# A two-layer hybrid trunk: the RWKV preparation spread into even steps with a third stage, and the weight split and own-shift product moved to other engines

## The chip, the cores and the metric

The kernel runs on one core of a Trainium2 chip. TensorE (PE) does the matrix products, VectorE (DVE), ScalarE (ACT) and GpSimd (POOL) the element work, and SyncE (SP), ACT and POOL issue DMAs. The metric is the device time of one execution in microseconds (us); a kernel's time is the median of its runs. One execution of each kernel is also profiled, and all the rows below are of that execution.

## The reference, cut to what matters

Two layers run over 256 context tokens and 2048 latent tokens of width 1024. Each layer is, for all 2304 tokens:

```python
h = rms_norm(x, norm_w[l]) * (1.0 + scale) + shift        # scale, shift, gate from SiLU(c) @ mod_w
pa, pb, pt = _split(h @ w_in[l], (RWKV_COLS, HGRN_COLS, ATTN_COLS))
pa = pa + mu_prev * (prev(pa) - pa) + mu_next * (next(pa) - pa)      # centred_shift, RWKV columns only
...                                                       # RWKV-7, HGRN2 and windowed attention
x = x + gate * (jnp.concatenate([ya, yb, yt], axis=-1) @ w_out[l])
```

In the RWKV group a state of 64 by 64 for each of 6 heads and 2 directions is stepped through all tokens. The kernel does that in chunks of 64 tokens. For each chunk it needs products of decays, two triangular 64 by 64 matrices and the inverse of a unit triangular one, and these depend on the features alone, not on the state.

## The kernel before, in words

A layer has two phases. `inproj_phase` computes `h @ w_in`; `phase2` runs the three mixers and the output projection. The program's instructions are put in an order on each engine by a scheduler that works through the program as written and has a timing model of its own; an instruction that stands earlier in the program goes first when several could go. Each engine then executes its list strictly in that order, so what the scheduler placed too early makes the engine wait.

**The input projection.** The 4096 columns of `w_in` are worked in 32 columns of 128 (33 in layer 1, which has one more for `vw1`), in two sweeps over the tokens: sweep 0 has three groups of tokens (512, 256 and 512), sweep 1 has two of 512. For each position of a sweep `prefetch` splits the next column's weights `wraw` into `whi` and `wlo` (`split`, L307 to L314: a cast and a subtraction on POOL), and has POOL issue the load of the column after that into the one `wraw` buffer. `group` (L339) then runs 24 matmuls into a PSUM tile `ps` and has ACT empty it. For the 14 RWKV columns (`j < 14`, "shifted") ACT writes a padded row buffer `pb`, of which there is one, and `end` (L379) makes the centred shift out of it on DVE: `s = pb * mu0` (L391, `self.ts`), then two `self.stt` that add the neighbours' shares. For the other columns ACT writes `s` directly. Of `s` there are two buffers; `post` works on `s` and stores it to scratch in HBM.

**The preparation** (`RwkvPrep`, L608) makes the chunks' products window by window, 256 tokens each, 9 windows a layer, 5 in sweep 0 and 4 in sweep 1. `fronts` loads `th` (by an SP DMA from scratch `wa`) and `lr`, `lk`, `lkk`, casts `th` to `tk` (L699), multiplies by `wa` into PSUM `aps` on PE, goes through tanh, a scan and exponentials, forms `tk` and `lkk`, stores them, and multiplies them into the triangular matrices `M`. `backs` sends the diagonal 32 by 32 blocks of `M` through HBM (scratch `Lx`) into `inv` and `can`, inverts them by a chain of 60 small DVE instructions, copies the results on ACT, sends them through HBM again (scratch `Dx`, the writes on ACT's queue, the reads into `XT` and `daT` on SP's), and completes the inverse by two sets of 48 matmuls with operands of 32 by 32 each (as many for either direction): first `G = apm<-daT,M`, copied by ACT to `Gs`, then `apm<-XT,Gs`. `XT` goes to scratch `XD`.

Both are generators that `yield` between pieces. `advance` (L654) runs one piece of the back of one window and one of the front of another. `behind` (L400), called after every position, opens the preparation after position 9 of sweep 0 and adds the sweep's windows there, and calls `advance` `CFG["pa"]` = 6 times a position. Before, a window's front has five pieces for each direction, and its back five in all.

**Modulation.** In layer 0 the later shifts and gates (`later_modulation`) are computed among the first positions, at a priority lowered by `CFG["mo"]` = 1000 places. The preparation can be opened only when the modulation has released its PSUM and SBUF.

**Phase 2** is a merge of generators for the RWKV state, HGRN, attention and read-out. Attention begins by finishing what is left of the preparation and then takes its memory.

Of the kernel before, what the change touches and what calls it, by code (L numbers as in the profile page):

```python
# [17 lines left out]

CFG = dict(og=0, eg=0, ib=2, lo=0, xb=4, hf=3, np=3, tm=4, pa=6, ch=1, pq=2, wps=2, ahead=100, he=92, ae=86, re=105, mo=1000, hd=1, wq=2, rq=0, oq=0, rl=500, nx=0, nl=2, bl=2, xa=0, od=3, g1=0, g2=0, g3=0, b2=0, b3=0)
L = 2  # L20
# [22 lines left out]
def W(ap, n):  # L43
    return ap[:, n:n + 1]


class Trunk:
# [227 lines left out]
    def inproj_phase(self, l, src, prep, start):  # L275
# [7 lines left out]
        with ExitStack() as ph:  # L283
# [23 lines left out]
            def split(n):  # L307
                if n < len(seq):
                    w = raw.pop(n)
                    hi = wsp.tile([128, KD, 128], F32R, name="whi", tag="whi")  # L310
                    lo = wsp.tile([128, KD, 128], F32R, name="wlo", tag="wlo")
                    nc.gpsimd.tensor_copy(hi, w)  # L312
                    self.tt(lo, w, hi.bitcast(F32), ALU.subtract, nc.gpsimd)
                    spl[n] = (hi, lo)  # L314
# [24 lines left out]
            def group(sw, n, st, t0, bn, every):  # L339
# [17 lines left out]
                if not shifted:  # L357
                    self.evac(l, j, s[:, t0 - base:t0 - base + bn], ps[:, 0:bn], t0 - base, bn)
                else:
                    o = t0 - base + (1 if t0 == 0 or sw else 2)  # L360
                    if c0 == 0:
                        self.act(pb[:, o:o + bn], ps[:, 0:bn], AF.Identity)
                    if t0 == 0:
                        self.act(pb[:, 1282:1283], ps[:, BLK:BLK + 1], AF.Identity)

            edge = (nc.gpsimd, nc.vector)[CFG["eg"]]
# [12 lines left out]
            def end(sw, n, st):  # L379
# [3 lines left out]
                if shifted:  # L383
# [3 lines left out]
                    else:  # L387
                        segs = [(1280, 1024, 1)]
                    m0, mp, mn = W(self.mu0[l], j), W(self.P(l, "mup"), j), W(self.P(l, "mun"), j)
                    for t0, bn, c in segs:  # L390
                        sv = s[:, t0 - base:t0 - base + bn]  # L391
                        self.ts(sv, pb[:, c:c + bn], m0, ALU.mult)
                        self.stt(sv, pb[:, c - 1:c - 1 + bn], mp, sv, ALU.mult, ALU.add)
                        self.stt(sv, pb[:, c + 1:c + 1 + bn], mn, sv, ALU.mult, ALU.add)
# [5 lines left out]
            def behind(sw, pos):  # L400
                if sw == 0 and pos < 7:
                    next(start, None)
                if pos == 9:
# [204 lines left out]
class RwkvPrep:  # L608
# [3 lines left out]
    def __init__(self, t, l, ph):  # L612
        self.t, self.l, self.nc, self.ph = t, l, t.nc, ph
        self.todo, self.ready, self.done, self.front, self.back = [], [], set(), None, None

# [38 lines left out]
    def advance(self):  # L654

        if not self.front and self.todo:
            w = self.todo.pop(0)
            self.front = [w, self.fronts(w)]
        if not self.back and self.ready:
            w = self.ready.pop(0)  # L660
            self.back = [w, self.backs(*w)]
        if not (self.front or self.back):
# [12 lines left out]
    def fronts(self, w):  # L675
# [7 lines left out]
        def load():  # L683
            for n in ("r", "k", "kk"):
# [3 lines left out]
                nc.sync.dma_start(out=d[n], in_=S[n][:, :, t0:t0 + 256].rearrange("i p t -> p i t"))  # L688
        M = T_([128, 6, 4, 64], "M", 2)
        v3 = lambda a: a.rearrange("p i (c s) -> p (i c) s", s=64)  # L690
        f3 = lambda a: a.rearrange("p (c s) -> p c s", s=64)
        for z in range(2):
# [53 lines left out]
            nc.sync.dma_start(out=S["KB"][z, 4 * w:4 * w + 4].rearrange("c p i s -> p i c s"), in_=tk.rearrange("p (i c) f s -> p i c (f s)", c=4))  # L746
            for p0, pn in ((0, 2), (2, 1)):
                ps = self.ps([128, 8, 64])
# [11 lines left out]
    def backs(self, w, M):  # L760
# [5 lines left out]
        for z in range(2):  # L766
            for g, b in enumerate((0, 1) if z == 0 else (1, 0)):
# [15 lines left out]
        for j in range(1, 31):  # L783
# [3 lines left out]
            t.tt(i3[:, j + 1:32, 0:j], i3[:, j + 1:32, 0:j], tv, ALU.subtract)  # L787
        yield

# [3 lines left out]
        Dx = S["Dx"]  # L793
        daT = T_([128, 12, 32], "daT")
        for q in range(4):
# [5 lines left out]
            for hp in range(2):  # L801
# [3 lines left out]
                if g == 0:  # L805
                    nc.sync.dma_start(out=daT[rb], in_=Dx[4 + z, 12 * hp:12 * hp + 12].rearrange("u r c -> r u c"))
        yield

        G = self.pm.tile([128, 12, 32], F32, name="apm", tag="apm")
        Gs = T_([128, 384], "Gs").rearrange("p (u s) -> p u s", s=32)  # L810
        q4 = lambda hp, i: slice(64 * hp + 32 * i, 64 * hp + 32 * i + 32)
        for z in range(2):
            a, b = (0, 1) if z == 0 else (1, 0)
            for u in range(12):
                p, c = divmod(u, 4)
                for hp in range(2):
                    t.mm(G[q4(hp, b), u], M[q4(hp, a), 3 * z + p, c, 32 * b:32 * b + 32], daT[q4(hp, a), u])
        t.act(Gs, G, AF.Identity)
        yield
        O = self.pm.tile([128, 12, 32], F32, name="apm", tag="apm")  # L820
        for z in range(2):
            a, b = (0, 1) if z == 0 else (1, 0)
            for u in range(12):
                p, c = divmod(u, 4)
                for hp in range(2):
                    t.mm(O[q4(hp, a), u], Gs[q4(hp, b), u], XT[q4(hp, b), 3 * z + p, c, 32 * b:32 * b + 32])
        for z in range(2):
# [823 lines left out]
```

## Time and profile before

| | |
|---|---|
| median of 3 runs | 4546.02 us (4545.11 to 4547.92) |
| the profiled execution | 4540.61 us, span of the trace 4538.8 us |
| TensorE busy with matmuls / with weight loads | 3941.3 us (87%) / 3217.7 us (71%) |
| VectorE / ScalarE / GpSimd busy | 3164.2 us (70%) / 1984.9 us (44%) / 1390.9 us (31%) |
| mean granted TensorE clock | 0.929 of full speed |

Layer 0's input projection lies from the start to about 1230 us, its phase 2 to about 2290 us, layer 1's input projection to about 3495 us, and its phase 2 to the end. The preparation runs from about 350 to 800 us (sweep 0) and from 800 to 1230 us (sweep 1) in layer 0, and from 2500 to 2960 us and from 3160 to 3495 us in layer 1. The shares are averages over these stages; what the change touches is read from the input projections.

### The profile page before, as it was taken

To read this page: it belongs to the slowest core of one execution; us is meant where nothing else is said; L and a number is where in the kernel's file an instruction comes from. 1 tells how busy PE (TensorE), PEld (TensorE's weight loads), DVE (VectorE), ACT (ScalarE), POOL (GpSimd) and SP (SyncE) were. 2 spreads that over 40 slices of the span, in tenths; PEclk is the share of its full clock that TensorE was granted. 3 is DMA by queue.
4 is the path that set the end of the run, shared out by engine and by line. 5 is a ranking of instruction groups with operands and counts; after the bars stand their busy time and mean duration, and the time that the engine had idled before them with its cause. 6 is when DMAs were issued, how large, how long until landed. Compare 5 with 4: busy or idle time off the path is not lost. (4 is left out here: it accounts for less than half of the span.)

```text
span 4538.8 us, 98552 instructions
## 1 busy us (share of the span) xinstructions
PE 3941.3 (87%) x39424; PEld 3217.7 (71%) x39424; DVE 3164.2 (70%) x5646; ACT 1984.9 (44%) x4050; POOL 1390.9 (31%) x1298
## 2 busy tenths in 40 slices
PE   7998898889789889868979988898887888988788
PEld 4767776777677777766758767776676777777676
DVE  3547777678577887777744777556775877777786
ACT  3414343443355555533424353333433555555443
POOL 2322233223233332242243212243222422333232
PEclk8999898999899999988989989899898999999899
DMA  5466654666643334346634476435665543334554
GB/s 202 144 200 197 198 158 121 190 197 190 167 123 107 106 105 115 91 118 214 209 117 129 143 231 195 116 106 172 197 185 159 135 113 101 97 104 126 171 187 132
DMA packets 777312, 688.41 MB, mean 152 GB/s; under 512 B 352164, under 2 KB 675044, under 8 KB 776856
## 3 DMA queue, kind: packets, MB, share of 16 engines
q1 hardware_dynamic: 747624, 583.93, 43.4%
q0 software_dynamic: 18720, 68.17, 5.2%
q10 hardware_dynamic: 10512, 30.02, 2.0%
q8 instruction: 312, 5.11, 0.5%
q14 instruction: 144, 1.18, 0.1%
HBM read 440.70 MB, written 241.22 MB: 150 GB/s over the span
## 5 line engine op out<-in xcount | busy, mean ns | idle before, releaser
L67 PE MATMUL ps<-h,whi 128*128 128x512 f32 x4160 | 1374.7, 406 | 18.2 <-ACT s L64 11.2
L67 PEld LDWEIGHTS ps<-h,whi 128*128 128x128 f32 x4160 | 806.0, 195 | 207.7 <-issue 19.5
L67 PE MATMUL ps<-h,wlo 128*128 128x512 f32 x2080 | 850.9, 409 | 5.2 <-POOL wlo L74 5.2
L312 POOL CAST whi<-wraw 128x1024 fp32r<-128x1024 f32 x130 | 151.6, 1166 | 1124.0 <-PE ps L67 991.8
L67 PEld LDWEIGHTS ps<-h,wlo 128*128 128x128 f32 x2080 | 411.7, 198 | 95.4 <-POOL wlo L74 6.3
L74 POOL TENSOR_TENSOR hE<-hb 128x256 f32<-128x256 f32 x408 | 290.9, 735 | 326.7 <-PE wps L67 195.7
L74 POOL TENSOR_TENSOR wlo<-wraw,whi 128x1024 fp32r<-128x1024 f32 x130 | 335.3, 2579 | 10.5
L1085 DVE COPY_PREDICATED hatt<-lm,wps 64x256 f32<-64x256 int32 x476 | 266.7, 560 | 29.8 <-PE wps L67 23.2
L64 ACT ACT_TABLE_LOAD x177 | 227.1, 1283 | 109.9 <-DVE s L79 33.4
L74 DVE TENSOR_TENSOR Gs<-can,inv 128x30 f32<-128x30 f32 (+9 forms) x540 | 238.9, 442 | 35.0 <-PE apm L67 23.7
L67 PE MATMUL pq<-KZ,BKs 128*64 128x128 f32 x2496 | 228.2, 297 | 34.9 <-DMA KZ<-scr_RK 18.8
L67 PE MATMUL opo<-wohi,ohi 128*128 128x512 f32 x544 | 216.2, 413 | 31.2 <-DVE og L74 18.6
L74 DVE TENSOR_TENSOR hQz<-hE,hqz 128x512 f32<-128x512 f32 x204 | 179.8, 882 | 76.4 <-DMA hqz<-scr_hq 67.8
L74 DVE TENSOR_TENSOR inv<-inv,Gs 128x30 f32<-128x30 f32 (+9 forms) x540 | 223.5, 414 | 12.1
L83 DVE SCALAR_TENSOR_TENSOR s<-pb,par,s 128x1024 f32<-128x1024 f32 (+1 forms) x156 | 217.3, 1393 | 5.6
L67 PE MATMUL opo<-wolo,ohi 128*128 128x512 f32 x544 | 212.9, 407 | 0.0
L64 ACT ACTIVATE pt<-wps 128x512 f32<-128x512 f32 (+1 forms) x288 | 149.4, 525 | 137.1 <-PE wps L71 132.7
L67 PEld LDWEIGHTS pq<-KZ,BKs 128*64 128x64 f32 x2496 | 169.4, 147 | 53.6 <-issue 19.8
L64 ACT ACTIVATE s<-ps 128x512 f32<-128x512 f32 (+1 forms) x175 | 95.8, 562 | 251.6 <-PE ps L67 222.8
L64 ACT ACTIVATE pb<-ps 128x512 f32<-128x512 f32 (+2 forms) x162 | 77.1, 492 | 290.5 <-PE ps L67 204.1
L71 PE MATMUL wps<-ident,prob 128*128 128x128 f32 x960 | 168.7, 292 | 40.8 <-DVE hatt L1085 22.8
L79 DVE TENSOR_SCALAR s<-pb,mu 128x1024 f32<-128x1024 f32 (+1 forms) x78 | 62.1, 796 | 194.7 <-ACT pb L64 193.9
(272 smaller groups left out, 9225.8 us busy)
## 6 DMA issues: line engine op xcount, KB each, us to landing
wraw<-in_w_in_dram POOLq DMA_DIRECT2D x128, 512.0 KB, 4.6
scr_KB<-tk SPq DMA_DIRECT2D x36, 768.0 KB
BKs<-scr_KB SPq DMA_DIRECT2D x144, 192.0 KB
KZ<-scr_RK SPq DMA_DIRECT2D x272, 96.0 KB
x<-in_mod_w_dram SPq DMA_DIRECT2D x32, 512.0 KB
lkk<-scr_kk SPq DMA_DIRECT2D x36, 384.0 KB
th<-scr_wa SPq DMA_DIRECT2D x36, 384.0 KB
scr_RK<-lkk SPq DMA_DIRECT2D x36, 384.0 KB
```

What stands on the lines that cost most here:

```text
L64: return self.nc.scalar.activation(out=out, in_=in_, func=func, **kw)
L67: return self.nc.tensor.matmul(out=out, lhsT=lhsT, rhs=rhs, start=start, stop=stop)
L71: return self.nc.tensor.transpose(out, in_, self.ident[0:p, 0:p])
L74: return (eng or self.nc.vector).tensor_tensor(out=out, in0=a, in1=b, op=op)
L79: return e.tensor_scalar(out=out, in0=a, scalar1=s1, scalar2=None, op0=op0)
L83: return (eng or self.nc.vector).scalar_tensor_tensor(out=out, in0=a, scalar=s, in1=b, op0=op0, op1=op1)
L312: nc.gpsimd.tensor_copy(hi, w)
L1085: nc.vector.copy_predicated(o, m, d)
```

## The change

Five things change.

1. **Where the preparation's steps stand.** `advance` is called once after each `group` (three a position in sweep 0, two in sweep 1) and, by `behind`, one time more a position in sweep 1, so that a position has 3 calls and not 6, and they stand between its groups and not after it.
2. **Its pieces.** A front has six pieces for each direction and not five (the products into `M` are a piece of their own). The 60 instructions of the inversion are cut into pieces after `j` = 6, 12, 18, 24 and 30. What follows the second trip through HBM (`G`, its copy, the last products and the store to `XD`) becomes a third generator, `tails`, which `advance` runs beside the next window's back; it begins with four empty pieces, and there are two between `G` and the last products. `G`'s copy goes into free blocks of `M` and not into `Gs`.
3. **The weight split** goes from POOL to ACT (`whi`) and DVE (`wlo`).
4. **The own-shift product** `s = pb * mu0` goes from DVE (from `pb`, 128x1024 and 128x256 at a time, after the last group) to ACT (from PSUM, after each group).
5. **The later modulation** is lowered by 300 places and not by 1000.

```diff
-                    nc.gpsimd.tensor_copy(hi, w)
-                    self.tt(lo, w, hi.bitcast(F32), ALU.subtract, nc.gpsimd)
+                    self.act(hi, w, AF.Identity)
+                    self.tt(lo, w, hi.bitcast(F32), ALU.subtract)
...
                     if c0 == 0:
                         self.act(pb[:, o:o + bn], ps[:, 0:bn], AF.Identity)
+                        self.act(s[:, t0 - base:t0 - base + bn], ps[:, 0:bn], AF.Identity, scale=W(self.mu0[l], j))
...
+                prep.advance()
...
-                        self.ts(sv, pb[:, c:c + bn], m0, ALU.mult)
                         self.stt(sv, pb[:, c - 1:c - 1 + bn], mp, sv, ALU.mult, ALU.add)
                         self.stt(sv, pb[:, c + 1:c + 1 + bn], mn, sv, ALU.mult, ALU.add)
...
-                for _ in range(CFG["pa"]):
+                for _ in range(3 - (2 if sw or last and order[pos] in free else 3)):
                     prep.advance()
...
+        if self.tail and next(self.tail[1], 1) == 1:
+            self.done.add(self.tail[0])
+            self.tail = None
         if self.back and next(self.back[1], 1) == 1:
-            self.done.add(self.back[0][0])
+            self.tail = [self.back[0][0], self.tails(*self.back[0], *self.back[2:])]
             self.back = None
...
             t.tt(i3[:, j + 1:32, 0:j], i3[:, j + 1:32, 0:j], tv, ALU.subtract)
-        yield
+            if j % 6 == 0:
+                yield
...
-        yield
-
+
+    def tails(self, w, M):
+
+        t, nc, S = self.t, self.nc, self.t.scr
+        XT, daT = self.XT, self.daT
+        yield
+        yield
+        yield
+        yield
         G = self.pm.tile([128, 12, 32], F32, name="apm", tag="apm")
-        Gs = T_([128, 384], "Gs").rearrange("p (u s) -> p u s", s=32)
+        blk = lambda r, z, e: M[r, 3 * z:3 * z + 3, :, 32 * e:32 * e + 32]
...
-        t.act(Gs, G, AF.Identity)
+
+        for z in range(2):
+            b = 1 - z
+            for hp in range(2):
+                t.act(blk(q4(hp, b), z, b), G[q4(hp, b)].rearrange("s (p c) t -> s p c t", c=4), AF.Identity)
+        yield
         yield
```

What this does to the order of instructions is shown at three places.

On ACT, in layer 0's first sweep, the emptying of the RWKV column 4 (`pb_1292` before, `pb_1295` after). Before, each group has one instruction for `pb`:

```order
L64 ACTIVATE pb_1292<-ps_1295 128x512
L64 ACTIVATE pb_1292<-ps_1321 128x256
L64 ACTIVATE pb_1292<-ps_1321 128x1
L64 ACTIVATE t_1382<-s_1294,par0_91 128x256
L64 ACTIVATE pb_1292<-ps_1348 128x512
```

After:

```order
L64 ACTIVATE pb_1295<-ps_1298 128x512
L64 ACTIVATE s_1297<-ps_1298,mu0_0_104 128x512
L64 ACTIVATE pb_1295<-ps_1325 128x256
L64 ACTIVATE s_1297<-ps_1325,mu0_0_104 128x256
L64 ACTIVATE pb_1295<-ps_1325 128x1
L64 ACTIVATE t_1386<-s_1297,par0_91 128x256
L64 ACTIVATE pb_1295<-ps_1353 128x512
L64 ACTIVATE s_1297<-ps_1353,mu0_0_104 128x512
L64 ACTIVATE whi_1419<-wraw_1293 128x1024
```

Every group has a second pass for `s`, and the next column's cast follows the last group's passes.

On DVE, in the same sweep, the shift of column 6 (`s_1744` before, `s_1890` after; `th`, `lr` and `pc` belong to a front, `scanm` is the scan's mask). Before, with the next column's shift behind it:

```order
L79 TENSOR_SCALAR s_1744<-pb_1742,mu0_0_104 128x256
L83 SCALAR_TENSOR_TENSOR s_1744<-pb_1742,par0_91,s_1744 128x256 x2
L79 TENSOR_SCALAR s_1744<-pb_1742,mu0_0_104 128x1024
L83 SCALAR_TENSOR_TENSOR s_1744<-pb_1742,par0_91,s_1744 128x1024 x2
L79 TENSOR_SCALAR s_1972<-pb_1970,mu0_0_104 128x256
```

After:

```order
L83 SCALAR_TENSOR_TENSOR s_1890<-pb_1888,par0_91,s_1890 128x256 x2
L80 TENSOR_SCALAR th_1958<-th_1958 128x768
L728 SCALAR_TENSOR_TENSOR th_1958<-scanm_1854,th_1958 128x256 x3
L74 TENSOR_TENSOR lr_1920<-lr_1920,P_1874 128x768
L746 COPY pc_146<-P_1874 128x3x4
L83 SCALAR_TENSOR_TENSOR s_1890<-pb_1888,par0_91,s_1890 128x1024
L74 TENSOR_TENSOR wlo_2047<-wraw_1886,whi_2046 128x1024
L83 SCALAR_TENSOR_TENSOR s_1890<-pb_1888,par0_91,s_1890 128x1024
```

The preparation's work begins earlier, among the shifted columns, and `wlo` stands in the same list.

On PE, the products `G` (`apm<-daT,M`) of layer 0's first window. Before:

```order
L67 MATMUL ps<-h,whi 128x512
L71 MATMUL pa<-ident,s 128x128 x8
L67 MATMUL ps<-h,whi 128x512
L67 MATMUL apm<-daT,M 32x32
L67 MATMUL ps<-h,whi 128x512
L67 MATMUL ps<-hc,whi 128x256
L67 MATMUL ps<-hc,wlo 128x256
L67 MATMUL apm<-daT,M 32x32 x24
L67 MATMUL aps<-tk,wa_1849 128x256 x6
```

After, the same window's, all 48 in one run:

```order
L67 MATMUL ps<-h,wlo 128x512
L67 MATMUL ps<-h,whi 128x512 x4
L67 MATMUL apm<-daT,M 32x32 x48
L71 MATMUL pa<-ident,s 128x128 x8
L67 MATMUL ps<-h,whi 128x512 x4
```

After, the third window's:

```order
L67 MATMUL ps<-h,whi 128x512
L67 MATMUL apm<-daT,M 32x32
L67 MATMUL ps<-h,wlo 128x512
L67 MATMUL ps<-h,whi 128x512
L67 MATMUL ps<-h,wlo 128x512
L67 MATMUL apm<-daT,M 32x32 x47
```

Where the scheduler put the first of the 48 alone and the rest some rows later, it placed each as soon as its model had the operand landed. Before, that is so in 16 of the 18 windows; after, in 13. The six matmuls `aps<-tk` that open the two halves of a direction's front come, counted in runs of 24 matmuls of `ps` over 512 columns, every 4.2 such runs before and every 5.5 after in layer 0's first sweep, every 3.5 and 5.2 in layer 1's first, and every 4.3 and 4.9, and 3.8 and 4.6, in the second sweeps. The last window's tail of each layer falls into phase 2.

## Rows read from the trace of the kernel before

**Rows 1.** Busy time by stretch, header first; clock as granted, (x) instructions.
```profile
core 0: us, PE busy (x) PEld busy (x) DVE busy (x) ACT busy (x) POOL busy (x), PEclk, DMA share, GB/s
...
50.00:350.00 300.00, 292.14 (x1407) 214.25 (x1407) 142.39 (x184) 104.23 (x168) 86.36 (x82) 0.98 0.53 166
350.00:800.00 450.00, 389.81 (x2968) 326.21 (x2966) 335.23 (x635) 184.91 (x303) 126.65 (x98) 0.90 0.58 169
800.00:1230.00 430.00, 382.22 (x3024) 314.12 (x3026) 309.44 (x527) 175.12 (x274) 123.78 (x105) 0.90 0.61 184
...
2500.00:2960.00 460.00, 402.97 (x3163) 335.18 (x3162) 321.63 (x606) 179.96 (x296) 105.58 (x87) 0.90 0.57 169
2960.00:3160.00 200.00, 182.44 (x832) 140.24 (x832) 112.50 (x126) 76.86 (x117) 84.72 (x76) 0.96 0.46 140
3160.00:3495.00 335.00, 280.47 (x2147) 226.37 (x2142) 232.98 (x444) 125.63 (x187) 85.98 (x67) 0.89 0.59 174
```

**Rows 2.** PE's waits over the span: us in total, times, longest us.
```profile
PE apm L67 <- DMA daT<-scr_Dx: 67.7, 36, 8.1
...
PE pa L71 <- DVE hf L80: 42.5, 40, 9.7
PE aps L67 <- DVE tk L74: 33.8, 11, 9.8
PE aps L67 <- DVE tk L699: 29.7, 14, 4.1
...
PE ps L67 <- POOL wlo L74: 5.2, 3, 2.0
```

**Rows 3.** PE's timeline around 604 us: start, duration, instruction, [idle before <- releaser].
```profile
603.87 1.62 PE L67 MATMUL aps<-tk,wa 128*128 128x256 f32 x6 [3.99 <-DVE tk L699]
...
608.06 0.63 PE L67 MATMUL ps<-h,whi 128*128 128x512 f32 x1
608.49 0.63 PE L67 MATMUL ps<-h,wlo 128*128 128x512 f32 x1
...
611.21 0.39 PE L67 MATMUL ps<-h,wlo 128*128 128x512 f32 x1
611.44 0.39 PE L67 MATMUL ps<-h,whi 128*128 128x512 f32 x1
```

**Rows 4.** Busy time by stretches of 4 us there, columns as in rows 1.
```profile
600.00:604.00 4.00, 0.13 (x1) 0.16 (x1) 1.91 (x3) 0.00 (x0) 3.62 (x3) 0.82 1.11 375
604.00:608.00 4.00, 4.00 (x19) 4.00 (x20) 3.72 (x10) 1.21 (x3) 0.37 (x1) 0.50 0.56 149
608.00:612.00 4.00, 4.00 (x18) 3.29 (x17) 3.90 (x10) 1.20 (x2) 0.00 (x0) 0.83 0.00 0
```

**Rows 5.** DVE's timeline there, columns as in rows 3.
```profile
602.10 1.63 DVE L699 CAST tk<-th 128x512 fp32r<-128x512 f32 x1 [3.00 <-DMA th<-scr_wa]
```

**Rows 6.** The page's costliest groups: count | busy us, mean ns | idle before, releaser.
```profile
L312 POOL CAST whi<-wraw 128x1024 fp32r<-128x1024 f32 x130 | 151.6, 1166 | 1124.0 <-PE ps L67 991.8
...
L74 POOL TENSOR_TENSOR wlo<-wraw,whi 128x1024 fp32r<-128x1024 f32 x130 | 335.3, 2579 | 10.5
...
L79 DVE TENSOR_SCALAR s<-pb,mu 128x1024 f32<-128x1024 f32 (+1 forms) x78 | 62.1, 796 | 194.7 <-ACT pb L64 193.9
```

**Rows 7.** Instructions on the tile tk: ns of one, least/median/most.
```profile
L74 DVE TENSOR_TENSOR tk<-tk,th x72: 939/950/3126, 355.4 to 3373.5; 128x768 f32<-128x768 f32 x72
L699 DVE CAST tk<-th x36: 408/427/2648, 332.7 to 3346.6; 128x512 fp32r<-128x512 f32 x36
```

**Rows 8.** Groups of ACT instructions by line and shape, columns as in rows 6.
```profile
L64 ACT ACTIVATE s<-ps 128x512 f32<-128x512 f32 x148 | 86.8, 595 | 224.3 <-PE ps L67 195.5 <-DMA scr_aq<-s 12.3 <-DMA scr_sgr<-s 8.1
...
L64 ACT ACTIVATE wohi<-wo 128x1024 fp32r<-128x1024 f32 x16 | 16.8, 1052 | 21.1 <-DMA wo<-in_w_out_dram 21.0
```

**Rows 9.** Waits of ACT and DVE over the span, columns as in rows 2.
```profile
ACT pb L64 <- DVE s L83: 82.2, 15, 11.8
...
DVE tk L699 <- DMA th<-scr_wa: 63.5, 21, 7.3
```

More of the change, by code (lines that the diff above doesn't have):

```diff
@@ L17 @@
 PSUM = bass.MemoryType.PSUM
-CFG = dict(og=0, eg=0, ib=2, lo=0, xb=4, hf=3, np=3, tm=4, pa=6, ch=1, pq=2, wps=2, ahead=100, he=92, ae=86, re=105, mo=1000, hd=1, wq=2, rq=0, oq=0, rl=500, nx=0, nl=2, bl=2, xa=0, od=3, g1=0, g2=0, g3=0, b2=0, b3=0)
+CFG = dict(og=0, eg=0, ib=2, lo=0, xb=4, hf=3, np=3, tm=4, ch=1, pq=2, wps=2, ahead=100, he=92, ae=86, re=105, mo=300, hd=1, wq=2, rq=0, oq=0, rl=500, nx=0, nl=2, bl=2, xa=0, od=3, g1=0, g2=0, g3=0, b2=0, b3=0)
 L = 2
@@ L388, in end @@
                         segs = [(1280, 1024, 1)]
-                    m0, mp, mn = W(self.mu0[l], j), W(self.P(l, "mup"), j), W(self.P(l, "mun"), j)
+                    mp, mn = W(self.P(l, "mup"), j), W(self.P(l, "mun"), j)
                     for t0, bn, c in segs:
                         sv = s[:, t0 - base:t0 - base + bn]
-                        self.ts(sv, pb[:, c:c + bn], m0, ALU.mult)
                         self.stt(sv, pb[:, c - 1:c - 1 + bn], mp, sv, ALU.mult, ALU.add)
@@ L613, in __init__ @@
         self.t, self.l, self.nc, self.ph = t, l, t.nc, ph
-        self.todo, self.ready, self.done, self.front, self.back = [], [], set(), None, None
+        self.todo, self.ready, self.done, self.front, self.back, self.tail = [], [], set(), None, None, None
     def open(self):
@@ L661, in advance @@
             self.back = [w, self.backs(*w)]
-        if not (self.front or self.back):
+        if not (self.front or self.back or self.tail):
             return False
+        if self.tail and next(self.tail[1], 1) == 1:
+            self.done.add(self.tail[0])
+            self.tail = None
         if self.back and next(self.back[1], 1) == 1:
-            self.done.add(self.back[0][0])
+            self.tail = [self.back[0][0], self.tails(*self.back[0], *self.back[2:])]
             self.back = None
@@ L688, in load @@
                 nc.sync.dma_start(out=d[n], in_=S[n][:, :, t0:t0 + 256].rearrange("i p t -> p i t"))
-        M = T_([128, 6, 4, 64], "M", 2)
         v3 = lambda a: a.rearrange("p i (c s) -> p (i c) s", s=64)
@@ L746, in fronts @@
             nc.sync.dma_start(out=S["KB"][z, 4 * w:4 * w + 4].rearrange("c p i s -> p i c s"), in_=tk.rearrange("p (i c) f s -> p i c (f s)", c=4))
+            yield
+            if z == 0:
+                M = T_([128, 6, 4, 64], "M", 2)
             for p0, pn in ((0, 2), (2, 1)):
@@ L793, in backs @@
         Dx = S["Dx"]
-        daT = T_([128, 12, 32], "daT")
+        daT = self.daT = T_([128, 12, 32], "daT")
         for q in range(4):
@@ L817, in backs @@
                     t.mm(G[q4(hp, b), u], M[q4(hp, a), 3 * z + p, c, 32 * b:32 * b + 32], daT[q4(hp, a), u])
-        t.act(Gs, G, AF.Identity)
+        for z in range(2):
+            b = 1 - z
+            for hp in range(2):
+                t.act(blk(q4(hp, b), z, b), G[q4(hp, b)].rearrange("s (p c) t -> s p c t", c=4), AF.Identity)
+        yield
         yield
@@ L825, in backs @@
                 for hp in range(2):
-                    t.mm(O[q4(hp, a), u], Gs[q4(hp, b), u], XT[q4(hp, b), 3 * z + p, c, 32 * b:32 * b + 32])
+                    t.mm(O[q4(hp, a), u], blk(q4(hp, b), z, b)[:, p, c], XT[q4(hp, b), 3 * z + p, c, 32 * b:32 * b + 32])
         for z in range(2):
```

## The prediction

> **What bounds the kernel now.** I read the stretches first [rows 1], then what PE waited for [rows 2], then one wait closely [rows 3 to 5]. PE is the engine to watch: in the input projection's quiet part it is busy 292 of 300 us at a granted clock of 0.98. Wherever the preparation runs beside the projection it is not: PE idles 450 - 389.8 = 60.2, 430 - 382.2 = 47.8, 460 - 403.0 = 57.0 and 335 - 280.5 = 54.5 us, 219.5 us in 1675 us or 13%, and the clock there is 0.90, 0.90, 0.90 and 0.89 [rows 1]. DVE is busy 70 to 74% in these four stretches, 56% in the stretch from 2960 us, where PE idles 8.8%, and 47% in the one from 50 us, where PE idles 2.6%. So PE's losses go with DVE's load, and the waits say so too: 106.0 us of PE's waits end with a DVE instruction that feeds the preparation or the norm (42.5 + 33.8 + 29.7), and 67.7 us with the DMA that brings `daT` to G [rows 2].
>
> **What a wait costs.** At 603.87 us PE ends a wait of 3.99 us [rows 3]. The clock in the three stretches of 4 us there is 0.82, 0.50 and 0.83 [rows 4]. The lower level is 1.2 GHz, half of 2.4, so 2 x (1.44 + 4.0 + 1.36) / 2 = 6.8 us were spent at it, at most 1.4 of them idle; 5.4 us of work took twice as long as it need, 2.7 us lost. The spacing shows it: 0.43 us from one 512-column matmul to the next at 608.06, 0.23 us at 611.21 [rows 3]. A wait of 4 us thus costs 6.7 us, 1.67 per us. Over the four stretches the clock's mean leaves 2 x 10% of the time, some 342 us, at the lower level; if all idle time fell into it, 122 us of work ran at half rate (61 us lost), if none did, 171 us were lost. The one wait's ratio gives 219.5 x 0.67 = 147, inside that. Short waits may not lower the clock, so I take 1.5 per us of idle removed.
>
> The room by PE's busy time is the 219.5 us. The Trainium skill, "Perfetto Trace Analysis", section "Identifying the Most-Contended Engine", says that the matmul busy share is a poor measure for TensorE since matmuls are pipelined, and that the share of weight loads is a better one. By that the room in the four stretches is 1675 - 1201.9 = 473 us [rows 1]; its time stands under the rivals.
>
> **The change part by part.** *The weight split* takes 151.6 + 335.3 = 486.9 us off POOL [rows 6], which nobody waits for: PE waited 5.2 us for `wlo` [rows 2]. ACT gets 130 casts; the same cast of `wohi` takes 1052 ns [rows 8], 137 us. DVE gets 130 subtractions; a two-input one of 768 columns takes 939 ns at least [rows 7], so one of 1024 about 1.24 us (an estimate by columns), 161 us. *The own-shift product* leaves DVE, 62.1 us [rows 6], and costs ACT 134 passes of at most 595 ns [rows 8], some 75 us. Both ACT costs lie beside PE: ACT is busy 40% of the four stretches (665.6 of 1675 us) [rows 1], and would be near 49%. What stands behind them on ACT is the emptying of `ps`; PE has three such buffers.
>
> *DVE is slowed by POOL.* The same instruction takes 950 ns or 3126, 427 or 2648 [rows 7], and the cast in front of PE's wait above took 1.63 us while POOL was busy 3.62 of 4 us [rows 4, 5]; the 2.2 us between least and most are about one POOL subtraction (2.58 us [rows 6]). How much of 486.9 us of POOL's split was taken out of DVE no row sums up: none at least, all at most. Most instructions run near their least, so I take 200. DVE's balance is then -62 + 161 - 200 = -101 us (bounds +99 and -388).
>
> *The even steps* do the rest. The order shows that the half-direction fronts, 3.5 to 4.3 runs of matmuls apart before, are 4.6 to 5.5 apart after, about a fifth more time for the same preparation. Without it DVE has some 51% of the time to do (between the 47 and 56% of the quiet stretches), 860 of 1199 us in the four stretches, which leaves 339 us for the preparation; over 2010 instead of 1675 us that is 1032 + 339 - 101 = 1270 us, a load of 63%. The load of `th` gets a whole group between its issue and its use: DVE waited 63.5 us for it in 21 waits [rows 9], and PE behind DVE, as at 602.10 us [rows 5].
>
> *The tail.* Four empty pieces ahead of G are meant to have `daT` landed. The order shows that the scheduler still puts G at the first moment that its model allows in 13 windows of 18, before in 16. So 3 of 16 windows' waits go for certain, 13 us, and the others shrink only as the inversion in front of them ends earlier: 0 to 55 us; together I take 25 of 67.7, nearer to the certain part.
>
> *The sum of idle time removed.* By causes: 25 for G and 55% of 106.0, 58, makes 83 us. By load: from 56% to 72% of DVE the idle share rises from 8.8 to 13.1%; at 63% it is 10.7%, 2.4% of 2010 us, 48 us. I take 70, between them and nearer to the first, since G's part hangs little on load. Times 1.5: 105 us. Against it: a last tail in each phase 2, at 67.7 / 18 = 3.8 us a window, and the earlier modulation, the same work in the quiet part, where PE has 8 us idle: 0 to 10 us together, 5 taken. Profiled time 4540.6 - 100 = 4441; the median of the runs lies 5.4 us above the profiled execution, so 4446, say 4445.
>
> **The rivals.** *The contention was the root.* If DVE without POOL's split keeps up, most of the DVE-named waits go (80%, 85 us) and half of G's (34): 119 x 1.67 = 199 less 5, about 4352. For it: the 2.2 us blocks hit just the instructions that PE waits for. Against: G's places, and `th`'s DMA, are untouched by it. The same 32% of the room by weight loads (70 of 219.5) would be 151 of 473 us, 4395; so the rule of the Trainium skill gives, by this case's rows, a time at the edge of this rival, and shares its chance.
>
> *The change hardly does what it says.* The scheduler goes on placing the consumer at the earliest moment of its model, so each wait comes back at the next place. Then G's 13 us and a quarter of the DVE-named waits (26) go: 39 x 1.5 less 5 is 53, 4493; with half of that, 4520. For it: 13 of 18.
>
> *Slower.* `wlo` now stands in DVE's list behind instructions that wait, such as the cast of `th` (3.0 us a wait) and `pb`'s shift, which ACT waited 82.2 us for in 15 waits, 5.5 us each [rows 9]. Before, POOL had it ready long before (5.2 us of waiting in all). If `wlo` comes late, PE waits at the column's start, with all three `ps` buffers empty, and nothing hides it. The two projections have 130 columns in some 2400 us, 18.4 us each, so 91 of them in the four stretches; from 67 us of new idle time, 0.74 us a column, the gain is gone. At 1.2 us a column, 91 x 1.2 x 1.5 = 164 less 100, it is 4610. Against it: the split is ordered a column ahead, some 18 us, and the order puts `whi` just behind the last group's emptying.
>
> **How the numbers follow.** Main case, 4400 (the 83 us, each at 1.67 us, would give 4412) to 4490: 0.48. Contention the root, under 4400: 0.20. Hardly, 4490 to 4537: 0.14. No change within 0.2%, which is about what a measurement of this kernel can tell from none: 0.05. Slower: 0.13. Faster is 0.82. The range from 4350 leaves out about 0.07 below, where both the contention and G's waits would have to go; to 4530 it leaves out 0.15 above and takes in most of the third case. The unknown with the widest bounds is DVE's balance; its bad end belongs to the slower case, its good end to the second.
>
> **What would show it.** In the profile after: POOL down by some 480 us, to about 900; ACT up by about 210; DVE's total down by about 100, and the longest times of `tk<-th` and `tk<-tk,th` no longer 2.2 us above the least. PE's waits for `aps<-tk` halved, for `daT` still 40 us or so; the clock in the preparation's stretches 0.93 or more; phase 2's lengths (1060 and 1044 us) within 10 us of before. Wrong would be: a row "PE ps <- DVE wlo" of tens of us, ACT waiting for stores of `s`, or idle time of PE unchanged while DVE's load fell, which would say that the order and not the load sets the waits.

## The result: 4408.9 us, and nearly all of it by the split

The changed kernel takes 4408.9 us (4400.4 to 4419.4, 4 runs), the kernel before 4547.0 (4545.1 to 4548.5): a ratio of 0.9689, 95% interval 0.9666 to 0.9713, 138 us saved. The prediction said 4445 in a range of 4350 to 4530. The profiled execution took 4413.4 us with a span of 4411.5.

The gain lies in the two projections. Counted from the first to the last matmul into `ps`, the layers' projections took 48.3 to 1183.6 and 2336.4 to 3493.2 us before, and take 49.6 to 1118.9 and 2282.2 to 3354.0 us after: 66 and 85 us less. The phases behind them are 11 and 12 us longer.

The page's busy times of the kernel after: ACT rose from 1984.9 us, POOL fell from 1390.9 and DVE from 3164.2.

```profile
PE 3910.7 (89%) x39424; PEld 3192.5 (72%) x39424; DVE 2980.8 (68%) x5698; ACT 2207.8 (50%) x4368; POOL 901.7 (20%) x1038
```

Stretches of the kernel after, columns as in [rows 1]; the third and the last end with the projection.

```profile
50.00:350.00 300.00, 292.41 (x1500) 214.46 (x1499) 139.81 (x226) 140.02 (x229) 34.48 (x51) 0.98 0.58 183
350.00:800.00 450.00, 409.25 (x3167) 339.81 (x3168) 306.66 (x620) 245.35 (x384) 51.05 (x63) 0.94 0.58 172
800.00:1119.00 319.00, 298.44 (x2089) 244.50 (x2087) 221.05 (x435) 164.14 (x249) 22.83 (x36) 0.96 0.65 195
...
2500.00:2960.00 460.00, 412.92 (x3159) 335.49 (x3159) 310.36 (x644) 238.14 (x372) 37.79 (x55) 0.93 0.59 176
...
3160.00:3354.00 194.00, 179.18 (x1479) 147.47 (x1478) 142.96 (x309) 91.59 (x146) 12.04 (x20) 0.96 0.63 185
```

The quiet first stretch is as it was. In the four with preparation the clock is 0.93 to 0.96, and PE idles 8.7% (123.2 of 1423 us). [rows 1] has 0.89 or 0.90 and 13% for before, but its stretch from 800 us runs 46 us beyond the projection, whose last matmul into `ps` starts at 1183.6 and not near 1230 us. In those 46 us PE idles 14 us at a clock of 0.63. Up to 1184 us the kernel before has (columns as in [rows 1]):

```profile
800.00:1184.00 384.00, 350.25 (x2474) 286.02 (x2474) 284.97 (x474) 155.80 (x237) 117.04 (x96) 0.94 0.61 184
```

So that stretch stood at 0.94 before, and with it the four idled 12.6% (205.5 of 1629 us). The clock rose clearly in the other three.

PE's waits over the span after, as in [rows 2]:

```profile
PE pa L71 <- DVE hf L80: 47.6, 40, 10.8
PE apm L67 <- DMA daT<-scr_Dx: 41.3, 24, 4.3
...
PE aps L67 <- DVE tk L704: 9.9, 7, 2.2
...
PE ps L67 <- DVE wlo L74: 3.2, 4, 1.4
PE aps L67 <- DVE tk L74: 3.2, 3, 1.5
```

The two waits for `tk` fell from 63.5 to 13.1 us, those for `daT` from 67.7 to 41.3; those for `hf` did not fall. The new row, `ps` behind `wlo` on DVE, is as small as the one of POOL was.

The instructions on `tk`, ns least/median/most, as in [rows 7]:

```profile
L74 DVE TENSOR_TENSOR tk<-tk,th x72: 935/950/955, 283.3 to 3294.6; 128x768 f32<-128x768 f32 x72
L704 DVE CAST tk<-th x36: 408/426/430, 258.8 to 3273.6; 128x512 fp32r<-128x512 f32 x36
```

Least and median stand where they stood; the longest, 3126 and 2648 ns before, are gone. To see how much this is over all of DVE, I took for each line, operation and shape the duration at its tenth percentile as undisturbed, and added up what every instruction took above it. I call the sum DVE's delay. In the two projections it was 158 and 147 us before, and is 30 and 31 after. Another grouping of the shapes moves a figure by up to some 20 us, and the differences between kernels by about as much.

### The profile page after: what moved, and what is told of

Its sections match the earlier page's. It is cut to its first block, busy times and chain, and to the rows that moved or that the text cites. A ratio compares the mean times of both kernels' runs of the same rounds, so it can differ in the third digit from the quotient of the medians.

```text
span 4411.5 us, 98661 instructions
## 1 busy us (share of the span) xinstructions
PE 3910.7 (89%) x39424; PEld 3192.5 (72%) x39424; DVE 2980.8 (68%) x5698; ACT 2207.8 (50%) x4368; POOL 901.7 (20%) x1038
## 5 line engine op out<-in xcount | busy, mean ns | idle before, releaser
L67 PE MATMUL ps<-h,whi 128*128 128x512 f32 x4160 | 1359.6, 402 | 39.0 <-ACT s L64 21.5
L67 PEld LDWEIGHTS ps<-h,whi 128*128 128x128 f32 x4160 | 796.5, 192 | 229.8 <-ACT s L64 26.1
L304 POOL DMA_DIRECT2D wraw<-in_w_in_dram x128 | 68.9, 539 | 1596.6 <-DVE wlo L74 1333.6
L83 DVE SCALAR_TENSOR_TENSOR s<-pb,par,s 128x1024 f32<-128x1024 f32 (+1 forms) x156 | 164.5, 1055 | 151.5 <-ACT s L64 94.7
L74 DVE TENSOR_TENSOR wlo<-wraw,whi 128x1024 fp32r<-128x1024 f32 x130 | 159.0, 1223 | 77.5 <-ACT whi L64 76.8
L74 DVE TENSOR_TENSOR inv<-inv,Gs 128x30 f32<-128x30 f32 (+9 forms) x540 | 185.4, 343 | 11.5
L74 DVE TENSOR_TENSOR Gs<-can,inv 128x30 f32<-128x30 f32 (+9 forms) x540 | 183.0, 339 | 11.3
L64 ACT ACTIVATE hE<-hE 128x512 f32<-128x512 f32 x204 | 128.6, 632 | 115.4 <-POOL hE L74 110.1
```

The source lines that it names most:

```text
L64: return self.nc.scalar.activation(out=out, in_=in_, func=func, **kw)
L67: return self.nc.tensor.matmul(out=out, lhsT=lhsT, rhs=rhs, start=start, stop=stop)
L74: return (eng or self.nc.vector).tensor_tensor(out=out, in0=a, in1=b, op=op)
L83: return (eng or self.nc.vector).scalar_tensor_tensor(out=out, in0=a, scalar=s, in1=b, op0=op0, op1=op1)
L304: (nc.sync, nc.scalar, nc.gpsimd)[CFG["wq"]].dma_start(out=w, in_=io["vw1"][l - 1] if j == 32 else io["w_in"][l, j])
```

## The experiments

Three theories. A: POOL's split held DVE's instructions up, and PE waited for DVE. B: the even steps and the third stage made the gain, by order or by load. C: it is POOL's time and place in its queue, whatever it does there. All runs, each ratio against the kernel before on the same chip; delay is DVE's, in the first and second projection:

| kernel | us | ratio (95%) | delay |
|---|---|---|---|
| split moved, no more | 4425.9 | 0.9731 (0.9711 to 0.9752) | 35, 28 |
| steps and third stage, no more | 4537.6 | 0.9986 (0.9972 to 1.0001) | 163, 160 |
| after, split back on POOL | 4539.5 | 0.9983 (0.9968 to 0.9998) | 149, 149 |
| after, own shift back on DVE | 4399.6 | 0.9682 (0.9660 to 0.9703) | 35, 35 |
| after, POOL reads | 4575.9 | 1.0067 (1.0047 to 1.0086) | 125, 139 |
| after, POOL fills | 4450.6 | 0.9800 (0.9771 to 0.9829) | 48, 51 |
| before, only `whi` moved | 4487.1 | 0.9871 (0.9840 to 0.9903) | 138, 118 |
| before, only `wlo` moved | 4474.1 | 0.9843 (0.9819 to 0.9866) | 54, 48 |
| after, POOL reads aside | 4512.5 | 0.9941 (0.9926 to 0.9956) | 143, 126 |
| after, POOL fills aside | 4428.1 | 0.9756 (0.9737 to 0.9774) | 37, 35 |
| own shift on DVE, third stage later | 4393.6 | 0.9681 (0.9659 to 0.9704) | 38, 33 |
| that, and `hE` on DVE | 4391.1 | 0.9670 (0.9653 to 0.9686) | 34, 38 |

### One part at a time

**The split alone**, on the kernel before:

```
-                    nc.gpsimd.tensor_copy(hi, w)
-                    self.tt(lo, w, hi.bitcast(F32), ALU.subtract, nc.gpsimd)
+                    self.act(hi, w, AF.Identity)
+                    self.tt(lo, w, hi.bitcast(F32), ALU.subtract)
```

> The kernel before with the weight split alone moved (whi on ScalarE, wlo on VectorE). Theory A, the split on GpSimd held VectorE up and VectorE held TensorE up: VectorE's total falls by some 80 us (161 us of wlo added, about 240 us of delay gone), TensorE's waits for aps<-tk fall to half of 63 us or less, and the time falls by 60 to 100 us, to 4450 to 4490. Theory B, the density of the preparation's steps sets the waits, whatever VectorE's speed: VectorE's total falls as well, but the time falls by under 30 us, since the scheduler goes on placing the preparation's products as early as it can.

It took 4425.9 us, 120 less than before, and more than theory A had expected (60 to 100).

**The steps alone**: the kernel after, with the split back on POOL, the own shift back on DVE and the modulation's old place (`mo=1000`).

```
-                    self.act(hi, w, AF.Identity)
-                    self.tt(lo, w, hi.bitcast(F32), ALU.subtract)
+                    nc.gpsimd.tensor_copy(hi, w)
+                    self.tt(lo, w, hi.bitcast(F32), ALU.subtract, nc.gpsimd)
...
-                        self.act(s[:, t0 - base:t0 - base + bn], ps[:, 0:bn], AF.Identity, scale=W(self.mu0[l], j))
...
+                        self.ts(sv, pb[:, c:c + bn], m0, ALU.mult)
```

> The changed kernel with the split back on GpSimd, the own-shift product back on VectorE and the modulation's priority as before, so that the even steps and the third stage are all that differs from before. Theory A: 30 to 60 us faster than before, 4485 to 4515, with the longest times of VectorE's tk instructions still 2.2 us above the least. Theory B: 90 us faster or more, under 4455.

It took 4537.6 us. The interval of its ratio reaches 1.0001: no change that could be told from none, and less than either theory had expected of the steps. Some of PE's waits moved rather than went: those for `daT` and `tk` are shorter than before, those for `hf` longer, and 31.7 us ahead of `aps`, in which PE waited for nothing that the trace shows, were 13.6 before.

```profile
PE pa L71 <- DVE hf L80: 53.1, 37, 9.5
PE apm L67 <- DMA daT<-scr_Dx: 50.7, 25, 9.8
...
PE aps L67 <- issue: 31.7, 8, 6.0
...
PE aps L67 <- DVE tk L704: 19.4, 12, 3.7
...
PE aps L67 <- DVE tk L74: 11.1, 5, 3.7
```

**The kernel after with only the split back on POOL** (the first four lines of the diff above):

> The changed kernel with the weight split alone put back on GpSimd. Theory A: it loses 60 to 100 us of the 138, so 4470 to 4510. Theory B: it loses under 30 us, so under 4440.

4539.5 us: taking this one part back takes nearly the whole gain, 131 of 138 us, where theory A had expected 60 to 100.

**The kernel after with only the own shift back on DVE** (the last two lines):

> The changed kernel with the own-shift product alone put back on VectorE (62 us of VectorE's work in 78 instructions, some 134 passes less on ScalarE). Theory A: VectorE's load counts, 62 us are a quarter of what the split's move frees: 10 to 25 us slower than the changed kernel, 4419 to 4434. Theory B: the same within 10 us.

4399.6 us, ratio 0.9682 against 0.9689: nothing was lost. DVE's busy time over the two projections rose by 51 us (1386.2 against 1334.6) and the projections took 2128 us against 2141. So these 51 us of DVE's load do not set the time here, as theory B had expected. Against the split alone, from runs on the same chip, this kernel is 26 us faster; that is what the steps, the third stage and the earlier modulation bring once the split is off POOL.

### Does POOL's reading do it?

**POOL busy again where the split was.** The split stays on ACT and DVE; POOL works on the spent raw weight, and nobody reads the outcome. First with reads, then with fills:

```
                     self.tt(lo, w, hi.bitcast(F32), ALU.subtract)
+                    nc.gpsimd.tensor_copy(w, hi.bitcast(F32))
+                    self.tt(w, w, hi.bitcast(F32), ALU.subtract, nc.gpsimd)
```

> The kernel after, with GpSimd busy again where the split was: behind each weight's split it copies whi over the spent raw weight and subtracts whi from it there (two instructions of 128x1024 that nobody reads; in the kernel before the two instructions of the split took 1166 and 2579 ns there). The split itself stays on ScalarE and VectorE. Theory A (a GpSimd instruction that reads SBUF holds up VectorE's, and TensorE then waits for VectorE): the gain of about 137 us goes, 4510 to 4560 us, and the VectorE delay above each shape's fast durations is back near 150 us in each projection, from 30. Theory B (the gain came from where the split stands: a weight that is ready sooner, fewer waits of TensorE for the split, VectorE's order): the time stays within 20 us of 4409, since nothing waits for these two instructions but the next raw weight's load.

```
                     self.tt(lo, w, hi.bitcast(F32), ALU.subtract)
+                    for _ in range(4):
+                        nc.gpsimd.memset(w, 0.0)
```

> The same place on GpSimd, about the same time there (four fills of the spent raw weight, 128x1024 each; a fill of that size took 0.95 us in the kernel after, so 3.8 us against the split's 3.75 us), but they read nothing from SBUF. Theory A in its narrow form (it is GpSimd's reading that holds VectorE up): within 20 us of 4409, VectorE's delay near 30 us in each projection. Theory C (it is GpSimd's time, whatever it does there: its queue is in order, and the next raw load, the halo columns and the halves of h behind the split come 3.8 us later, or a fill holds VectorE up as a subtraction does): 4510 to 4560, as the kernel with reads.

4575.9 and 4450.6 us: POOL was busy 1433 and 1404 us, and the reads cost 125 us more. Two groups of DVE that run beside the projections show why (count | busy us, mean ns). In the kernel before, the first fence; with reads, the second; with fills, the third:

```profile
L74 DVE TENSOR_TENSOR Gs<-can,inv 128x30 f32<-128x30 f32 (+9 forms) x540 | 238.9, 442 | 35.0 <-PE apm L67 23.7
...
L83 DVE SCALAR_TENSOR_TENSOR s<-pb,par,s 128x1024 f32<-128x1024 f32 (+1 forms) x156 | 217.3, 1393 | 5.6
```

```profile
L74 DVE TENSOR_TENSOR Gs<-can,inv 128x30 f32<-128x30 f32 (+9 forms) x540 | 225.0, 417 | 12.0
...
L83 DVE SCALAR_TENSOR_TENSOR s<-pb,par,s 128x1024 f32<-128x1024 f32 (+1 forms) x156 | 188.3, 1207 | 130.5 <-ACT s L64 80.8 <-issue 27.5 <-ACT pb L64 10.6
```

```profile
L74 DVE TENSOR_TENSOR Gs<-can,inv 128x30 f32<-128x30 f32 (+9 forms) x540 | 185.8, 344 | 11.7
...
L83 DVE SCALAR_TENSOR_TENSOR s<-pb,par,s 128x1024 f32<-128x1024 f32 (+1 forms) x156 | 164.6, 1055 | 140.9 <-ACT s L64 88.0 <-ACT pb L64 20.5 <-issue 18.9
```

In the kernel after they take 339 and 1055 ns: fills leave them as they are; reads bring back three quarters of what the first had lost since before, and somewhat under half of what the second had. The tile `tk` says what each does to one instruction (ns least/median/most). With reads:

```profile
L79 DVE TENSOR_SCALAR tk<-th,bones x72: 334/346/2477, 252.1 to 3425.0; 128x256 fp32r<-128x256 f32 x72
L74 DVE TENSOR_TENSOR tk<-tk,th x72: 939/949/3092, 287.6 to 3447.5; 128x768 f32<-128x768 f32 x72
```

With fills:

```profile
L79 DVE TENSOR_SCALAR tk<-th,bones x72: 333/348/1198, 250.9 to 3301.3; 128x256 fp32r<-128x256 f32 x72
L74 DVE TENSOR_TENSOR tk<-tk,th x72: 946/951/959, 284.9 to 3321.7; 128x768 f32<-128x768 f32 x72
L706 DVE CAST tk<-th x36: 410/427/1306, 250.5 to 3300.7; 128x512 fp32r<-128x512 f32 x36
```

Beside reads, instructions of one input and of two are both held up, by 2.1 us, some four fifths of a POOL subtraction (2541 ns there). Beside fills, the one with two inputs shown here never is (959 ns at most), while those with one are, by up to 0.9 us, about one fill (979 ns). The Trainium skill, "SBUF — State Buffer", section "Who interferes with whom", has a rule for this: VectorE shares a pair of ports with GpSimd, and whichever instruction has it first holds it to its end; a VectorE instruction with two inputs from SBUF contends with a GpSimd instruction that reads SBUF and not with one that only writes it, and copies, casts and scalar products can contend with GpSimd when they run in a two-port mode. These rows agree with it.

The kernel with reads came out 30 us above the kernel before, so something else is in it. Its PE waits show it:

```profile
PE ps L67 <- ACT whi L64: 51.7, 28, 4.4
...
PE ps L67 <- DVE wlo L74: 42.1, 32, 3.5
```

With fills the first of these is 18.5 us, in the kernel after 6.8: POOL issues the raw weight's load behind the extra work, so weights came late in both kernels. The kernel with fills lies between what the narrow theory A (4389 to 4429) and theory C (4510 to 4560) had expected. The next pair leaves the late weights out.

**The same behind the issue of the load**, on a small tile of its own:

```
                     load(n + 1)
+                    hi = spl[n][0].rearrange("p k c -> p (k c)").bitcast(F32)
+                    jk = wsp.tile([128, 256], BF16, name="wjk", tag="wjk", bufs=1)
+                    for a in range(0, 1280, 256):
+                        b = a % 1024
+                        self.tt(jk, hi[:, b:b + 256], hi[:, 768 - b:1024 - b], ALU.subtract, nc.gpsimd)
```

> The kernel after, with GpSimd reading SBUF beside the projections, but behind the issue of the next raw weight's load, so that no load comes later: per weight five subtractions of two quarters of whi (128x256 each, some 0.7 us by the row of hE, so about 3.6 us per weight and 465 us over the span), into a small tile that nobody reads. Contention (theory A): VectorE's delay above the fast durations rises from 30 to 80 to 150 us in each projection, and the time to 4490 to 4550 us. If the earlier kernel with reads lost its time by the late loads instead (its TensorE waited 94 us for whi and wlo): 4409 to 4435 us.

```
...
+                    nc.gpsimd.tensor_copy(jk[:, 0:1], hi[:, 0:1])
+                    for _ in range(13):
+                        nc.gpsimd.memset(jk, 0.0)
```

> The same place with fills only, a copy of one column and thirteen fills of the small tile (some 2 to 4 us per weight), behind the issue of the load. If the 42 us that the earlier kernel with fills lost came from the raw loads that it made late: 4400 to 4420 us. If they came from what stands behind on GpSimd's queue (halves of h, halo columns), or from the fills' writing: 4440 to 4455 us.

4512.5 and 4428.1 us, 84 apart, with nearly the same time on POOL. The reads, then the fills with their copies:

```profile
L74 POOL TENSOR_TENSOR wjk<-whi 128x256 bf16<-128x256 f32 x650 | 673.0, 1035 | 1086.1 <-ACT whi L64 1048.9 <-ACT tk L64 6.9
```

```profile
L324 POOL MEMSET wjk<- 128x256 bf16 x1690 | 546.7, 324 | 85.9
...
L322 POOL CAST wjk<-whi 128x1 bf16<-128x1 f32 x130 | 79.5, 612 | 976.3 <-ACT whi L64 972.4 <-ACT pb L64 3.7
```

PE waited 18.1 us for `whi` and `wlo` beside the reads and 18.8 beside the fills, so no weight came later for the reads. `Gs` took 402 ns beside the reads and 343 beside the fills. One by one these reads are longer than these fills, but that is not what parts them: the first fills took 979 ns each, about as long, and DVE's delay beside them is 99 us in the two projections, against 269 beside the reads. So reading, in a place where it makes no weight later, costs 84 us more than filling and brings back most of DVE's delay. Theory A holds for the larger part. Theory C keeps a smaller one, and 4428.1 lies between the two times expected (up to 4420, from 4440): the fills cost 19 us here against the kernel after, 30 by the ratios (0.9756 against 0.9689), and with late loads 42, or 50 by the ratios.

**What an idle us of PE costs.** The sums over the two projections, each from first to last matmul into `ps`: of the kernel before, of the kernel after, with reads, with fills, with reads aside and with fills aside, in this order:

```profile
sum 2293.00, PE 2049.11 PEld 1648.63 DVE 1511.64 ACT 896.93 POOL 666.29; mean PE 1024.55 PEld 824.31 DVE 755.82 ACT 448.46 POOL 333.15
```

```profile
sum 2141.00, PE 1988.29 PEld 1598.08 DVE 1334.62 ACT 1108.44 POOL 194.34; mean PE 994.14 PEld 799.04 DVE 667.31 ACT 554.22 POOL 97.17
```

```profile
sum 2318.00, PE 2056.53 PEld 1637.32 DVE 1583.43 ACT 1104.91 POOL 705.80; mean PE 1028.27 PEld 818.66 DVE 791.72 ACT 552.46 POOL 352.90
```

```profile
sum 2177.00, PE 2002.39 PEld 1604.70 DVE 1381.29 ACT 1111.71 POOL 685.96; mean PE 1001.20 PEld 802.35 DVE 690.64 ACT 555.86 POOL 342.98
```

```profile
sum 2259.00, PE 2039.13 PEld 1629.46 DVE 1559.26 ACT 1102.20 POOL 826.22; mean PE 1019.57 PEld 814.73 DVE 779.63 ACT 551.10 POOL 413.11
```

```profile
sum 2145.00, PE 2000.05 PEld 1604.10 DVE 1349.28 ACT 1108.34 POOL 796.43; mean PE 1000.02 PEld 802.05 DVE 674.64 ACT 554.17 POOL 398.22
```

PE idles 243.9, 152.7, 261.5, 174.6, 219.9 and 145.0 us. Reads against fills (the same number of matmuls, within one): 86.9 us more idle and 54.1 more busy, 1.62 us for each idle one. Reads aside against the kernel after (within three): 67.2 and 50.8, 1.76. Reads aside against fills aside (within nine): 74.9 and 39.1, 1.52. The extra busy time goes with the granted clock, 0.93 and 0.91 in the two projections with reads, 0.96 and 0.93 with fills.

### Which half of the split

**Only `whi` to ACT**, then **only `wlo` to DVE**, on the kernel before:

```
-                    nc.gpsimd.tensor_copy(hi, w)
+                    self.act(hi, w, AF.Identity)
```

> The kernel before, with only the copy whi on ScalarE; the subtraction wlo stays on GpSimd. If the delay of VectorE goes by GpSimd's time in the split, 151.6 of the 486.9 us leave, and of the 120 us that moving both brought, 37 come: about 4509 us. If only an instruction with two inputs holds VectorE up, nothing comes: 4535 to 4555. If the gain hangs on the copy, 4440 or less.

```
-                    self.tt(lo, w, hi.bitcast(F32), ALU.subtract, nc.gpsimd)
+                    self.tt(lo, w, hi.bitcast(F32), ALU.subtract)
```

> The kernel before, with only the subtraction wlo on VectorE; the copy whi stays on GpSimd. By GpSimd's time 335.3 of the 486.9 us leave, and of the 120 us some 83 come: about 4463 us. If only an instruction with two inputs holds VectorE up, all of the 120 come: 4415 to 4435. If VectorE's added 159 us of wlo costs more than the relief, 4540 or more.

58 and 72 us less than before; together 130, where both at once brought 120, so the halves add up. The time lies between what POOL's time and the copy alone would have made of the first (4509, and 4440 or less), and 11 us above what POOL's time would have made of the second (4463). That only POOL's two-input instruction does harm is out. But the gains don't go by DVE's delay alone: the copy took 49 us of it away and brought 58 us, the subtraction took 203 away, put 160 us of work on DVE and brought 72. Why the copy weighs so much is not settled. It stood at the head of POOL's queue and waited there for PE to release its buffer, 991.8 us in all [rows 6], and the halves of `h` and the halo columns stood behind it. That wait did not go with it: with only the copy moved, POOL waited longer still at the subtraction, for the `whi` that ACT writes there.

```profile
L74 POOL TENSOR_TENSOR wlo<-wraw,whi 128x1024 fp32r<-128x1024 f32 x130 | 359.1, 2762 | 1335.5 <-ACT whi L64 1271.2 <-PE ps L67 52.2 <-PE aps L67 12.1
```

### Can more be had?

**The third stage four groups later**, with the own shift on DVE:

```
         XT, daT = self.XT, self.daT
+        yield
+        yield
+        yield
+        yield
         yield
...
```

> The kernel after with the own shift weight back on VectorE (4399.6 us) and eight empty pieces instead of four ahead of the third stage's first matmuls, so that G stands four groups later behind the transfers that it needs. TensorE's waits for daT, 37.4 us in 21 there, should fall to under 15, worth 20 to 35 us at 1.0 to 1.5 us each: 4365 to 4385. Rival: G then stands beside other waits, or the later third stages pile up at the end of the projections: 4395 to 4415.

PE's waits for `daT` fell from 37.4 to 27.3 us, less than expected (under 15), and the time did not move: ratio 0.9681 against 0.9682.

**`hE` to DVE** in the phases behind the projections, on top of that:

```
-            t.tt(ex[:, :, z], ref, bx[:, :, z], ALU.subtract, nc.gpsimd)
-            t.tt(ex[:, :, sec], bx[:, :, sec], ref, ALU.subtract, nc.gpsimd)
+            t.tt(ex[:, :, z], ref, bx[:, :, z], ALU.subtract)
+            t.tt(ex[:, :, sec], bx[:, :, sec], ref, ALU.subtract)
```

> The kernel with the later third stage (4393.6 us), and in the phase behind each projection the two subtractions of the decays into hE, 128x256 each, on VectorE in place of GpSimd (283 us in 408 instructions there). It asks whether the lesson of the split holds where the receiving engine is VectorE itself. VectorE takes 408 instructions more, at some 0.33 us each by the nearest rows (asg 285 ns at 128x128, tk 349 ns at 128x256), 135 us; its delay above the fast durations in those two phases, 141 and 119 us, should fall by about half, 130 us, since the 283 us are nearly half of GpSimd's time there. If the delay sits where TensorE waits (for hatt 72 us in all), the time falls: 4350 to 4385. If VectorE's load is what TensorE waits for there, nothing comes or it is lost: 4390 to 4420.

4391.1 us, ratio 0.9670 against 0.9681, the intervals one over the other: nothing that can be told. The added group is dearer than estimated, 447 ns instead of 330:

```profile
L74 DVE TENSOR_TENSOR hE<-hb 128x256 f32<-128x256 f32 x408 | 166.1, 447 | 4.8
```

and DVE's delay in those two phases fell from 141 and 119 to 116 and 100 us, 44 instead of 130. 166 us of work bought 44 of delay; DVE's busy time there rose by 92 us (1646.8 to 1739.0). It is the lowest median of all, but its interval overlaps that of the kernel after (0.9666 to 0.9713), so no version here is shown to beat it. Of the delay that the kernel after has left in the projections, all 20 instructions that took over 0.15 us more than the median of their shape, 17 us in all, ran beside another subtraction on POOL, `h<-hf,h`; what moving that one would bring was not tried.

## Why the prediction was right, and where it was wrong

The direction held, and 4409 lies in the range and in the main case, 36 us under the number. That it lies in the main case is in part luck. The main case entered POOL's contention as a part of DVE's balance, let the even steps do the rest, and never split the gain between them; the split alone brought 120 us and the steps alone nothing that can be told, as the rival "the contention was the root" had it. One term too small and one too large offset each other. Of the row for `hf` [rows 2], this is what the first projection of before held (columns as there):

```profile
PE pa L71 <- DVE hf L80: 11.7, 11, 3.5
```

By the prediction's steps:

- *The split costs nothing where it went.* Right. ACT rose by 223 us (212 forecast), `wlo` on DVE took 1223 ns (1.24 us estimated), POOL fell to 902 us (900 forecast), and PE's wait for `wlo` was 3.2 us, 5.2 before. PE's waits ahead of `ps` for `s`, `h`, `whi` and `wlo` came to 24.4 us before and to 24.3 with the split alone. The mechanism of the slower rival did not appear. For the own shift it is less sure that ACT's passes lie beside PE: these waits are 41.2 us in the kernel after, and 28.4 with the own shift back on DVE, though the time did not show it.
- *What POOL's split took out of DVE*, 200 us of a possible 487: right in kind, low in size. DVE's delay in the projections fell by 244 us. DVE's total fell by 183 us where 101 was forecast, so by the forecast's own balance (-62 + 159 - 280) the term of 200 measured 280.
- *The even steps do the rest.* This step failed. Alone they changed nothing that could be measured; on top of the split they brought 26 us of the 138. The load of `th`, which was to get a whole group between issue and use, still keeps DVE waiting: 50.7 us in 19 waits, longest 9.5, and 63.5 in 21 before [rows 9].
- *The reckoning by load* (63% of DVE, PE idle 10.7%, 48 us) failed too: DVE was 69% busy in the four stretches after, and PE idled 8.7%. 51 us of DVE's work put back moved nothing. Its second point, 72% of DVE and 13.1% idle, rested on the stretch that ran to 1230 us: up to 1184 us DVE was 74% busy and PE idled 8.8%, as it did where DVE was 56% busy. The runs fit better with single instructions in front of a matmul that take up to 2 us longer. The forecast had that row in hand [rows 5, 7], and then used it only as a part of DVE's balance.
- *55% of the DVE-named waits.* Their total fell from 106.0 to 60.7 us, 43%, but not evenly: the two for `tk` by 79%, the one for `hf` not at all. I had read the row for `hf` over the whole span [rows 2] as if it belonged to the four stretches. Of its 42.5 us the first projection held 11.7 and the second 8.5, more than half stood outside both, and the four stretches held 10.4.
- *G's waits*, 25 us of 67.7: right, 26.4 went.
- *Idle removed, 70 us; price 1.5 us each.* The first was low. PE's idle time over the two projections fell from 243.9 to 152.7 us, 91 us, though part of that is work that moved out of them, since the phases behind are 23 us longer in all. The price was 1.62, 1.76 and 1.52 in three pairs with like matmuls, so the runs do not decide between the 1.67 of the single wait [rows 3, 4] and the 1.5 that I put in its place; what was low is the idle time removed.
- *The clock 0.93 or more, phase 2 within 10 us*: the first held, though one of the stretches had 0.94 before; the second missed by 1 and 2 us; where in those phases they went was not looked into.

The rival "the contention was the root" named the cause and put the time 57 us too low: it gave the waits for `hf` to the contention as well. The reading by weight loads of the Trainium skill, "Perfetto Trace Analysis", section "Identifying the Most-Contended Engine", gave 4395 and so came nearer, but by a share that the trace does not bear out: over the projections the time without a weight load fell from 644 to 543 us, 16%, not the 32% that went into it; in the four stretches, before's with its 46 us too many, it fell from 473 to 356 us, 25%.

## What to carry to other kernels

Look at the longest duration of an instruction, beside its median, before looking at an engine's load: here an engine that nobody waited for held up one that was waited for, and moving its work away was worth far more than its own waits. Test it by putting idle reads and idle fills in the same place. Before moving work onto the engine that suffers, weigh the work against the delay that goes with it: 160 us of `wlo`, moved alone, took 203 us of delay away and brought 72 us of time; 166 us of `hE` took 44 away and brought nothing that can be told.

## What the runs showed of the hardware that I had not expected

Fills on POOL held DVE up too, but nearly only instructions with one input. In the projections of the first kernel with fills, 52 instructions of one input and three of two took over 0.15 us more than the median of their shape with a fill as POOL's main instruction beside them. The hold goes with the length of POOL's instruction: the cast of `th` to `tk`, 427 ns, took at most 702 ns beside fills of 324 ns, 1306 beside fills of 979 ns, 1286 beside subtractions of 1035 ns and 2276 beside subtractions of 2541 ns.
